# Two transformer blocks on one Trainium2 core: a quarter of the block sums by an adding DMA, transposes three steps later, rotations on VectorE

## The chip, the cores and the metric

The kernel runs on one core of one Trainium2 chip. The core has five engines that each work through their own instructions in order and wait for each other by semaphores: TensorE (PE: matmuls and transposes), VectorE (DVE), ScalarE (ACT), GpSimd (POOL) and SyncE (SP, which here only issues DMAs). The metric is the device time of one execution in microseconds; less is better.

## What is computed

256 tokens of width 1024 go through two blocks of two layers each, all in fp32. Each layer is a gated feed-forward net, a token mixer, and a second feed-forward net, so there are eight feed-forward nets; the first block normalises with layer_norm, the second with rms_norm. The part that the change touches most is the feed-forward net, and of the second block's mixer the rotary step on the attention's queries and keys:

```python
def swiglu(x, w13, w2):
    a, b = jnp.split(x @ w13, 2, axis=-1)
    return (jax.nn.silu(a) * b) @ w2

def partial_rotary(t, positions):
    half = ROPE_DIM // 2
    ...
    t1 = t[..., :half].astype(jnp.float32)
    t2 = t[..., half:ROPE_DIM].astype(jnp.float32)
    rot = jnp.concatenate([t1 * cos - t2 * sin, t2 * cos + t1 * sin], axis=-1).astype(t.dtype)
    return jnp.concatenate([rot, t[..., ROPE_DIM:]], axis=-1)

def first_block(x, ...):
    ...
    for l in range(DEPTH):
        x = layer_norm(ALPHA * x + 0.5 * swiglu(x, ffn1_w13[l], ffn1_w2[l]), ln_g[l, 0], ln_b[l, 0])
        m = mixer(x, w_in[l], ...)
        x = layer_norm(ALPHA * x + m, ln_g[l, 1], ln_b[l, 1])
        x = layer_norm(ALPHA * x + 0.5 * swiglu(x, ffn2_w13[l], ffn2_w2[l]), ln_g[l, 2], ln_b[l, 2])
    return x
```

## The kernel before

**Tiling.** The tokens are two streams, i = 0 and 1, of 128 tokens. A product with weights is made of three matmuls in fp32r: each weight tile w is split into a rounded part wh and a rest wl, each input into xh and xl, and wh·xh, wl·xh and wh·xl are added up in one PSUM bank (128 x 512 fp32). Weights come as units of 128 x 1024 (512 KB). For each unit, `fetch` (L225) has SP load it four units ahead, and `split` (L258) has ACT round it to wh (L270) and DVE subtract to get wl (L273), a few units ahead of PE.

**A feed-forward net** is 84 units. The first two groups of hidden columns are computed for each stream on its own (`group`, L316), the rest for both streams together (`joint`, L455), and three *pairs* of groups stand among them (`pair`, L487). A pair multiplies a 2 x 2 block matrix of inputs (two streams, two halves of the width) by a 2 x 2 block matrix of weights ("11", "12", "21", "22") by the Strassen-Winograd scheme: seven products instead of eight, in the order p1, p2, q5, p3, p6, p7, q4, of two units and 12 matmuls (L545) each. There are 24 pairs in the program, three in each of the eight nets. The weights of four products are sums of blocks:

- q5 = p1's block + "12", p6 = q5 + "22", p7 = "22" + "12", q4 = p6 + "21".

`sum` (L240) makes each of them with one DVE add of 128 x 1024 a unit (L246), in place, when the unit before has been split: 8 adds a pair, 192 in all. The raw blocks, wh and wl are slots of one ring of 24 tiles (`whp`).

Between the products stand rows of the second weight matrix (`on`, L478, its matmuls at L300 into the banks called big), after p1, q5, p6 and p7 as given by `GAPS`. There are four PSUM banks for groups and products (pool `grp`): p1, p2 and q5 take one each; p3 adds on in q5's bank, and p6, p7 and q4 in p1's. So `after` (L519) copies a result with ACT (L499) before its bank is used again, and adds p2's bank into the copy of p1 with DVE (L502).

**Order around the change.** `later(n, fn)` puts `fn` off by n ticks of a clock that counts the units; with it, the transposes of what a group (`hidden`, sg, L438 to L449) or a pair (`hidden` within `pair`, kp, L509) has made are placed TURNS = 4 ticks later. In the attention's `rot` (L1011), POOL computes the rotation in six operations (L1021 to L1026) on queries aq and keys ak, and the transposes come 5 ticks later. SP and POOL work in the order of the program; the instructions of PE, DVE and ACT are put in order by a scheduler.

Of the kernel before, what the change touches and what calls it, by code (L numbers as in the profile page):

```python
# [11 lines left out]
F32 = mybir.dt.float32  # L12
# [3 lines left out]
ALU = mybir.AluOpType  # L16
# [3 lines left out]
P = 128  # L20
# [16 lines left out]
RAMP = 3  # L37
STEP = 1
TAIL = 2
PAIR = 5  # L40
LAGS = dict(ffn=9, mixer1=6, mixer2=6)
STAGES = 4
# [11 lines left out]

OWN = 2

TURNS = 4
FFN = (("g", 8), ("s", 2, 0, 1, 2, 3), ("g", 9), ("s", 4, 16, 17, 4, 5), ("g", 10), ("s", 6, 6, 7, 18, 19),
       ("r", 8), ("r", 9), ("r", 20), ("r", 21))
LAST = (10, 11, 12, 13, 14, 15)  # L60
# [19 lines left out]
class Core:  # L80
# [5 lines left out]
    def __init__(self, ctx, tc, a, out, order):  # L86
        self.tc, self.nc, self.a, self.out = tc, tc.nc, a, out
        self.order = order
        p = lambda n, b, **k: ctx.enter_context(tc.tile_pool(name=n, bufs=b, **k))
        self.cp = p("cp", 1)  # L90
        self.stg = p("stg", STAGES)
        self.whp = p("whp", 2 * RING)
        self.sp = p("sp", SLOTS)
        self.vp = p("vp", 2)
        self.st = p("st", 12)
        self.big = p("big", 4, space=PSUM)
        self.grp = p("grp", 4, space=PSUM)


        self.phase, self.made = [], []  # L100
        at = 0
        for what, _ in order:
            mixer = ("mixer1", 56) if what == "b1" else ("mixer2", 36)
            for kind, made in (("ffn", _ffn_units()), (mixer[0], list(range(mixer[1]))), ("ffn", _ffn_units())):
                self.phase += [(kind, m) for m in range(len(made))]
                self.made += [m + at if isinstance(m, int) else (*m[:2], m[2] + at) for m in made]
                at += FFN_ROWS if kind == "ffn" else len(made)
        self.nunit = len(self.made)
        self.raw = {}
        self.next_dma = self.next_split = 0  # L110
        self.stages, self.units = {}, {}
        self.n = 0
        self.clock = 0
        self.queue = []
        self.pos = [0, 0]
        self.x = [None, None]
        self.sh = {}
# [88 lines left out]
    def lead(self):  # L206
# [3 lines left out]
        left = dict(ffn=len(_ffn_units()), mixer1=56, mixer2=36)[kind] - n  # L210
        if self.product(min(self.pos[0] + PAIR, self.nunit - 1)):
            return PAIR
        return LEAD + (MORE if n < FIRST else max(0, MORE - left // RAMP))
# [23 lines left out]
    def block(self, b, u, base):  # L237
        return self.a["ws"][base + 2 * BLOCKS.index(b) + u]

    def sum(self, p, u, base):  # L240


        raw = self.raw

        def add(t, other):
            self.nc.vector.tensor_add(t, t, other)  # L246
            raw[p, u, base] = t

        if p == "q5":
            add(raw.pop(("p1", u, base)), raw["12", u, base])  # L250
        elif p == "p6":
            add(raw.pop(("q5", u, base)), raw["p3", u, base])
        elif p == "p7":
            add(raw.pop(("p3", u, base)), raw.pop(("12", u, base)))
        elif p == "q4":
            add(raw.pop(("p6", u, base)), raw.pop(("p2", u, base)))

    def split(self, u):  # L258
        while self.next_split <= min(u, self.nunit - 1):
            v = self.next_split  # L260
            self.fetch(v)
            made = self.made[v]
            product = self.product(v)
            w = self.raw[made] if product else self.stages.pop(v)
            hi = self.whp.tile([P, 1024], F32R, tag="w", name=self.nm("wh"))
            lo = self.whp.tile([P, 1024], F32R, tag="w", name=self.nm("wl"))
            halves = [slice(0, 512), slice(512, 1024)]
            wide = v >= 8 and self.phase[v][0] == "ffn"
            for h, c in enumerate([slice(0, 1024)] if wide else halves):
                r = self.nc.scalar.activation(hi[:, c], w[:, c], AF.Copy)  # L270
                if v < 3:
                    self.pin(r)
                self.nc.vector.tensor_sub(lo[:, c], w[:, c], hi[:, c])  # L273
            self.units[v] = [hi[:, c] for c in halves], [lo[:, c] for c in halves]
            self.next_split += 1
            self.fetch(v + STAGES)
            if self.next_split < self.nunit and self.product(v + 1):
                self.sum(*self.made[v + 1])

# [51 lines left out]
    def rows(self, i, ks, xT, accs, first, last):  # L331
# [3 lines left out]
        for k in ks:  # L335
            wh, wl = self.units[self.pos[i]]
            xh, xl = xT(k)
            both = k <= last - TAIL
            cs = (0, 1) if both else (0,)
# [93 lines left out]
    def hidden(self, J, i, acc, g):  # L433
# [18 lines left out]

        self.later(TURNS, turn)

# [32 lines left out]
    def pair(self, J, g, ks):  # L487
# [20 lines left out]
        def hidden(i, t, sg):  # L508
# [7 lines left out]

            self.later(TURNS, turn)

# [446 lines left out]
    def mixer2(self, i, rs, l):  # L965
        nc = self.nc
# [44 lines left out]
        def rot(name, scale):  # L1011
            def f(acc):
                t = self.slot(name=name)
                nc.scalar.activation(t, acc, AF.Identity, scale=rs)
                r = t.rearrange("p (h d) -> p h d", h=8)[:, :, 0:16].rearrange("p h (two e) -> p h two e", two=2)
                t1, t2 = r[:, :, 0, :], r[:, :, 1, :]
                cs = self.con[:, C_COS + 8 * i:C_COS + 8 * i + 8].unsqueeze(1).to_broadcast([P, 8, 8])
                sn = self.con[:, C_SIN + 8 * i:C_SIN + 8 * i + 8].unsqueeze(1).to_broadcast([P, 8, 8])
                w = self.slot((P, 4, 8, 8), name="rw")
                g = nc.gpsimd  # L1020
                g.tensor_tensor(w[:, 0], t1, cs, op=ALU.mult)  # L1021
                g.tensor_tensor(w[:, 1], t2, sn, op=ALU.mult)
                g.tensor_tensor(w[:, 2], t2, cs, op=ALU.mult)
                g.tensor_tensor(w[:, 3], t1, sn, op=ALU.mult)
                g.tensor_tensor(t1, w[:, 0], w[:, 1], op=ALU.subtract)
                g.tensor_tensor(t2, w[:, 2], w[:, 3], op=ALU.add)  # L1026

                def turn():
                    tp = self.transposed(t)
                    o = self.slot(name=name + "T")  # L1030
                    nc.scalar.activation(o, tp, AF.Copy, scale=scale)
                    J[name, i] = o

                self.later(5, turn)
            return f

        def av(acc):
# [424 lines left out]
def _ffn_units():  # L1462


    out, n = list(range(4 * OWN)), 4 * OWN
    for what, _, *ks in FFN:
        if what == "s":
            base, gaps = n, GAPS[len(GAPS) - len(ks):]
            n += 8
            for p in PRODUCTS:  # L1470
                out += [(p, u, base) for u in range(2)]
                if p in gaps:
                    out.append(n)
                    n += 1
        else:
            m = 4 if what == "g" else 1
            out += range(n, n + m)
            n += m
    return out + list(range(n, n + len(LAST)))
# [120 lines left out]
```

## Time and profile before

| | us |
|---|---|
| median of three runs | 2153.34 (2152.36 to 2153.6) |
| profiled execution | 2151.26 |
| its span, first to last instruction | 2149.5 |
| mean granted TensorE clock | 0.996 |
| PE busy | 2103.2 |
| DVE busy | 1849.6 |
| ACT busy | 1329.9 |
| POOL busy | 248.3 |
| DMA | 394.52 MB, 52.8% of the 16 engines' span |

How to read it: the span is the time from the first instruction to the last; the profiled execution's own time is longer by what lies around that. An engine's idle time costs something only where another engine waits for its next result. The granted clock is the share of full speed (2.4 GHz) that TensorE was given; 0.50 is the lower level, 1.2 GHz. A wait in the list of waits is idle time of an engine just before an instruction, put down to the line whose result came last. Times in the rows are microseconds from the span's start, and a row of the timeline gives the start and the duration of an instruction, or of several of one kind together (x4), and in brackets the idle time before it.

### The profile page before, as it was taken

What the parts mean: (1) busy time and instruction counts of PE and PEld (TensorE: products, weight loads), DVE (VectorE), ACT (ScalarE), POOL (GpSimd) and SP (SyncE); (2) the same over time, 40 slices, a digit from 0 to 9 for tenths busy, and PEclk for the clock granted to TensorE, in tenths of its full rate; (3) what the DMA queues carried; (4) which work ended last, traced back from release to release, by engine and by line L of the source; (5) the groups of instructions that cost most, each with busy time, mean ns of one, the idle gap of its engine ahead of it and who ended that gap; (6) DMA issues with size and microseconds to landing.
All of it is one profiled execution on the core that took longest, in us unless ns stands there. A gap on an engine that the chain in (4) does not pass through costs nothing.

```text
span 2149.5 us, 27945 instructions
## 1 busy us (share of the span) xinstructions
PE 2103.2 (98%) x9904; PEld 1730.3 (80%) x9904; DVE 1849.6 (86%) x2532; ACT 1329.9 (62%) x2040; POOL 248.3 (12%) x269
## 2 busy tenths in 40 slices
PE   8999999999999999999999999999999999999998
PEld 7887878888888887888888788788778878788887
DVE  7997787998899878699989988679988998777995
ACT  6665754666466575466656666756566666666663
POOL 0000420000000033001100201510200110241000
PEclk9999999999999999999999999999999999999999
DMA  8556455465554744546556454525554546343552
GB/s 313 187 191 239 138 184 172 161 240 193 200 194 177 232 154 164 189 163 228 194 195 216 176 196 133 177 98 197 208 196 173 186 181 211 122 158 117 204 189 98
DMA packets 115292, 394.52 MB, mean 184 GB/s; under 512 B 12880, under 2 KB 15312, under 8 KB 115152
## 3 DMA queue, kind: packets, MB, share of 16 engines
q1 hardware_dynamic: 115152, 392.73, 52.8%
q8 instruction: 78, 1.28, 0.2%
q14 instruction: 62, 0.51, 0.1%
HBM read 391.63 MB, written 1.05 MB: 183 GB/s over the span
## 4 chain that ended last, share of the span: by engine, by line
PE 81%; DVE 5%; issue 2%; ACT 2%; POOL 1%; DVEq 0%; POOLq 0%; ACTq 0%
PE g L300 32%; PE big L300 24%; PE g L545 18%; PE g L284 3%; DVE wl L273 2%; PE big L1254 1%; PE big L1283 1%; POOL rw L1021 1%; DVE raw L246 0%; ACT wh L270 0%; ACT xh L308 0%; PE big L1167 0%; PE big L1201 0%; PE big L793 0%; PE big L1173 0%
## 5 line engine op out<-in xcount | busy, mean ns | idle before, releaser
L273 DVE TENSOR_TENSOR wl<-stg,wh 128x512 fp32r<-128x512 f32 (+1 forms) x712 | 666.3, 957 | 122.6 <-ACT wh L270 114.1
L270 ACT ACTIVATE wh<-stg 128x512 fp32r<-128x512 f32 (+1 forms) x712 | 565.0, 823 | 222.2 <-DMA stg<-in_ws_dram 82.1
L300 PE MATMUL g<-wh,xh 128*128 128x512 f32 x1184 | 480.2, 406 | 9.6 <-ACT wh L270 5.6
L270 ACT ACTIVATE wh<-raw 128x1024 fp32r<-128x1024 f32 x336 | 352.3, 1058 | 196.9 <-DVE raw L246 106.6
L300 PE MATMUL g<-wl,xh 128*128 128x512 f32 x1184 | 464.9, 393 | 0.0
L300 PE MATMUL g<-wh,xl 128*128 128x512 f32 x1184 | 462.6, 392 | 0.7 <-DVE xl L309 0.7
L273 DVE TENSOR_TENSOR wl<-raw,wh 128x1024 fp32r<-128x1024 f32 x336 | 415.6, 1251 | 28.4 <-ACT wh L270 26.2
L300 PEld LDWEIGHTS g<-wh,xh 128*128 128x128 f32 x1184 | 223.5, 189 | 56.7 <-ACT xh L308 5.7
L300 PEld LDWEIGHTS g<-wh,xl 128*128 128x128 f32 x1184 | 223.4, 189 | 49.7 <-DVE xl L309 1.5
L300 PEld LDWEIGHTS g<-wl,xh 128*128 128x128 f32 x1184 | 224.0, 189 | 42.3 <-DVE wl L273 0.8
L246 DVE TENSOR_TENSOR raw<-raw,raw 128x1024 f32<-128x1024 f32 x192 | 233.0, 1231 | 5.5 <-DMA raw<-in_ws_dram 5.0
L300 PE MATMUL big<-wh,hT 128*128 128x512 f32 x640 | 183.9, 391 | 0.0
L545 PE MATMUL g<-wh,Xh 128*128 128x512 f32 x384 | 151.0, 394 | 1.7 <-ACT kp L499 1.4
L545 PE MATMUL g<-wl,Xh 128*128 128x512 f32 x384 | 150.2, 391 | 0.0
L545 PE MATMUL g<-wh,Xl 128*128 128x512 f32 x384 | 149.1, 390 | 0.0
L300 PEld LDWEIGHTS big<-wh,hT 128*128 128x128 f32 x640 | 119.5, 188 | 24.6
L300 PE MATMUL big<-wh,hTh 128*128 128x512 f32 x384 | 123.9, 390 | 0.0
L300 PE MATMUL big<-wh,hTl 128*128 128x512 f32 x384 | 123.8, 390 | 0.0
L300 PE MATMUL big<-wl,hTh 128*128 128x512 f32 x384 | 123.5, 389 | 0.0
L545 PE MATMUL g<-wh,xh 128*128 128x512 f32 x288 | 115.4, 401 | 0.0
L408 POOL TENSOR_TENSOR m<-m,nhalf 128x1 f32<-128x1 f32 (+1 forms) x24 | 25.5, 1065 | 761.2 <-DVE m L407 761.2
L545 PE MATMUL g<-wl,xh 128*128 128x512 f32 x288 | 113.1, 393 | 0.0
(319 smaller groups left out, 3045.0 us busy)
## 6 DMA issues: line engine op xcount, KB each, us to landing
stg<-in_ws_dram SPq DMA_DIRECT2D x519, 512.0 KB, 4.3
raw<-in_ws_dram SPq DMA_DIRECT2D x192, 512.0 KB, 4.7
row<-in_norm_gain_dram SPq DMA_DIRECT2D x24, 256.0 KB, 6.1
row<-in_ln_g_dram SPq DMA_DIRECT2D x12, 256.0 KB, 4.8
row<-in_ln_b_dram SPq DMA_DIRECT2D x12, 256.0 KB, 6.4
xT<-in_xT_dram SPq DMA_DIRECT2D x4, 256.0 KB, 5.9
x<-in_x_dram SPq DMA_DIRECT2D x4, 256.0 KB, 8.5
out_dram<-x SPq DMA_DIRECT2D x4, 256.0 KB, 2.0
```

The costliest lines, as they stand in the source:

```text
L246: self.nc.vector.tensor_add(t, t, other)
L270: r = self.nc.scalar.activation(hi[:, c], w[:, c], AF.Copy)
L273: self.nc.vector.tensor_sub(lo[:, c], w[:, c], hi[:, c])
L284: self.nc.tensor.transpose(tp[:, hs(j)], src[:, hs(j)], self.ident)
L300: self.nc.tensor.matmul(accs[c], a, b[c], start=start and q == 0, stop=stop and q == 2)
L408: self.nc.gpsimd.tensor_tensor(out, out, self.nhalf[:, 0:n], op=ALU.pow)
L545: nc.tensor.matmul(bank[p], x[:, hs(k)], w[j], start=first[p] == p and k + q == 0, stop=k == 3 and q == 2, skip_group_check=True)
L1021: g.tensor_tensor(w[:, 0], t1, cs, op=ALU.mult)
L1254: nc.tensor.matmul(ps[:, hh * S + j * P:hh * S + j * P + P], J["aq", i][r, hs(head // 2)], J["ak", j][r, hs(head // 2)], start=True, stop= ...
L1283: nc.tensor.matmul(o[:, 64 * hh:64 * hh + 64], pT[:, hs(2 * hh + j)], J["av", j][:, head * 64:head * 64 + 64], start=j == 0, stop=j == 1)
```

## The change

1. `added` is new. For each unit of p7, twelve units ahead (EARLY), SP loads block "12" into a tile of its own in the ring, and a DMA on POOL's queue adds block "22" to it from DRAM. The DVE adds of p7 go. q5 and p6 now give the raw blocks "12" and "22" back to the ring, since p7 doesn't use them.
2. TURNS goes from 4 to 7, for sg and kp.
3. The six operations of `rot` go from POOL to DVE, and their transposes come 4 ticks later instead of 5.

```diff
+EARLY = 12
...
-TURNS = 4
+TURNS = 7
...
+    def added(self, v):
+        if self.product(v) and self.made[v][0] == "p7":
+            _, u, base = self.made[v]
+            t = self.raw[self.made[v]] = self.whp.tile([P, 1024], F32, tag="w", name=self.nm("sum"))
+            self.nc.sync.dma_start(t, self.block("12", u, base))
+            self.nc.gpsimd.dma_start(t, self.block("22", u, base), accum_op=ALU.add)
...
         if p == "q5":
-            add(raw.pop(("p1", u, base)), raw["12", u, base])
+            add(raw.pop(("p1", u, base)), raw.pop(("12", u, base)))
         elif p == "p6":
-            add(raw.pop(("q5", u, base)), raw["p3", u, base])
-        elif p == "p7":
-            add(raw.pop(("p3", u, base)), raw.pop(("12", u, base)))
+            add(raw.pop(("q5", u, base)), raw.pop(("p3", u, base)))
...
             self.fetch(v + STAGES)
+            while self.next_sum < min(v + EARLY, self.nunit):
+                self.added(self.next_sum)
+                self.next_sum += 1
             if self.next_split < self.nunit and self.product(v + 1):
                 self.sum(*self.made[v + 1])
...
-                g = nc.gpsimd
+                g = nc.vector
...
-                self.later(5, turn)
+                self.later(4, turn)
```

In the changed kernel the lines past `split` are 11 further down (L545 is L556, L502 is L513), those ahead of it 2 to 10.

What it does to the order is shown at three places. The first is PE in one pair of the first net (g_5407 and g_5413 hold the transposes of sg, L284 before and L295 after; the products are at L545, now L556; g_5429 is p1's bank before, g_5447 and g_5484 are p2's and q5's now). Before, the transposes stand ahead of p1:

```order
L300 MATMUL big_5165<-wh_5320,hT_5272 128x512
L300 MATMUL big_5166<-wh_5320,hT_5272 128x512
L284 MATMUL g_5407<-con,sg_5363 128x128 x2
L284 MATMUL g_5413<-con,sg_5366 128x128 x2
L545 MATMUL g_5429<-wh_5326,xh 128x512
L545 MATMUL g_5429<-wl_5327,xh 128x512
```

and with the change between p2 and q5:

```order
L556 MATMUL g_5447<-wl_5375,xh 128x512
L556 MATMUL g_5447<-wh_5374,xl 128x512
L295 MATMUL g_5467<-con,sg_5393 128x128 x2
L295 MATMUL g_5473<-con,sg_5396 128x128 x2
L311 MATMUL big_5092<-wh_5437,hT_5224 128x512
L311 MATMUL big_5093<-wh_5437,hT_5224 128x512
L311 MATMUL big_5092<-wl_5438,hT_5224 128x512
L556 MATMUL g_5484<-wh_5399,Xh_5227 128x512
```

The transposes moved past p1 and p2 and took three matmuls of a row with them; before, q5's first matmul followed p2's last.

The second is SP's queue in a pair, from the load of "21" to that of "22" (raw is a block, stg a row's unit, sum the tile of the sum). Before:

```order
L234 DMA raw_4083<-in_ws_dram 128x1024
L234 DMA raw_4089<-in_ws_dram 128x1024
L234 DMA raw_4130<-in_ws_dram 128x1024
L231 DMA stg_4136<-in_ws_dram 128x1024
L234 DMA raw_4154<-in_ws_dram 128x1024
L234 DMA raw_4179<-in_ws_dram 128x1024
```

With the change:

```order
L236 DMA raw_4099<-in_ws_dram 128x1024
L236 DMA raw_4105<-in_ws_dram 128x1024
L236 DMA raw_4137<-in_ws_dram 128x1024
L247 DMA sum_4139<-in_ws_dram 128x1024
L233 DMA stg_4146<-in_ws_dram 128x1024
L247 DMA sum_4148<-in_ws_dram 128x1024
L236 DMA raw_4176<-in_ws_dram 128x1024
L236 DMA raw_4201<-in_ws_dram 128x1024
```

The two loads of "12" for the sum stand ahead of the loads of "22" (the last two rows), one on each side of the row's unit.

The third is the rotation of one stream's queries, before on POOL (rw and aq are its tiles):

```order
L1007 MEMSET vx_12067 128x4x4
L1021 TENSOR_TENSOR rw_12141<-aq_12139,con 128x64
L1022 TENSOR_TENSOR rw_12141<-aq_12139,con 128x64
L1023 TENSOR_TENSOR rw_12141<-aq_12139,con 128x64
L1024 TENSOR_TENSOR rw_12141<-aq_12139,con 128x64
L1025 TENSOR_TENSOR aq_12139<-rw_12141 128x8x8
L1026 TENSOR_TENSOR aq_12139<-rw_12141 128x8x8
```

and now on DVE:

```order
L281 TENSOR_TENSOR wl_12180<-stg_12051,wh_12179 128x512 x2
L1032 TENSOR_TENSOR rw_12201<-aq_12199,con 128x64
L1033 TENSOR_TENSOR rw_12201<-aq_12199,con 128x64
L1034 TENSOR_TENSOR rw_12201<-aq_12199,con 128x64
L1035 TENSOR_TENSOR rw_12201<-aq_12199,con 128x64
L281 TENSOR_TENSOR wl_12213<-stg_12091,wh_12212 128x512
L1036 TENSOR_TENSOR aq_12199<-rw_12201 128x8x8
L1037 TENSOR_TENSOR aq_12199<-rw_12201 128x8x8
L281 TENSOR_TENSOR wl_12213<-stg_12091,wh_12212 128x512
```

They stand among the subtractions that make wl (L281) and share their queue.

## Rows read from the trace of the kernel before

**Rows 1.** The page, part 1: busy time of each engine.
```profile
PE 2103.2 (98%) x9904; PEld 1730.3 (80%) x9904; DVE 1849.6 (86%) x2532; ACT 1329.9 (62%) x2040; POOL 248.3 (12%) x269
```
**Rows 2.** List of waits, PE: line, releaser, us in total, times, longest.
```profile
PE g L284 <- POOL aq L1026: 6.6, 2, 3.3
...
PE g L284 <- DVE kp L509: 5.1, 3, 2.1
PE g L284 <- DVE sg L443: 4.6, 3, 1.9
...
PE g L284 <- DVE sg L440: 1.7, 2, 0.9
```
**Rows 3.** Timeline, PE: start us, us, engine, line, operation, tiles [idle before].
```profile
1206.12 0.63 PE L284 MATMUL g<-con,kp 128*128 128x128 f32 x4 [2.07 <-DVE kp L509]
```
**Rows 4.** Windows at half clock: us, busy of each engine, clock, DMA share, GB/s.
```profile
1348.65:1352.06 3.41, 2.72 (x8) 1.92 (x8) 0.00 (x0) 0.60 (x1) 2.31 (x8) 0.50 0.31 118
1570.52:1573.93 3.41, 3.41 (x10) 2.64 (x9) 2.65 (x5) 1.47 (x3) 0.00 (x0) 0.50 0.00 0
1870.89:1881.13 10.24, 8.62 (x21) 6.03 (x22) 3.39 (x6) 5.15 (x11) 4.96 (x13) 0.50 0.36 120
```
**Rows 5.** Windows in one pair, busy of PE, PEld, DVE, ACT, POOL.
```profile
434.00:446.00 12.00, 12.00 (x57) 9.75 (x56) 11.43 (x13) 8.43 (x10) 0.00 (x0) 1.00 0.95 375
...
454.00:474.00 20.00, 20.00 (x92) 16.54 (x91) 19.97 (x21) 14.83 (x20) 0.00 (x0) 1.00 0.24 82
```
**Rows 6.** Groups by line and form, DVE: busy us, mean ns | idle before.
```profile
L246 DVE TENSOR_TENSOR raw<-raw,raw 128x1024 f32<-128x1024 f32 x192 | 233.0, 1231 | 5.5 <-DMA raw<-in_ws_dram 5.0
...
L1286 DVE TENSOR_SCALAR at<-big,m 128x64 f32<-128x64 f32 x32 | 8.2, 279 | 6.5 <-PE big L1283 6.3
```
**Rows 7.** Timeline, SP's DMA queue: the row unit's load in that pair.
```profile
440.06 0.36 SPq L231 DMA_DIRECT2D stg<-in_ws_dram  x1
```
**Rows 8.** DMA issues of 430 to 446: count, KB each, median us to landing.
```profile
raw<-in_ws_dram SPq DMA_DIRECT2D x7, 512.0 KB, 7.8
```
**Rows 9.** Timeline, ACT: q5's copy and a rounding in that pair.
```profile
465.09 0.60 ACT L499 ACTIVATE kq<-g 128x512 f32<-128x512 f32 x1 [0.96 <-PE g L545]
466.97 1.06 ACT L270 ACTIVATE wh<-raw 128x1024 fp32r<-128x1024 f32 x1 [1.28 <-DVE raw L246]
```
**Rows 10.** Timeline, PE: the first matmul of p3 in that pair.
```profile
467.61 0.39 PE L545 MATMUL g<-wh,Xh 128*128 128x512 f32 x1
```
**Rows 11.** Timeline, PE, another pair: transposes of sg, then p2 to its end.
```profile
501.24 0.60 PE L284 MATMUL g<-con,sg 128*128 128x128 f32 x4
501.60 0.49 PE L545 MATMUL g<-wh,xh 128*128 128x512 f32 x1
501.92 0.39 PE L545 MATMUL g<-wl,xh 128*128 128x512 f32 x1
...
504.23 0.39 PE L545 MATMUL g<-wh,xl 128*128 128x512 f32 x1
```
**Rows 12.** Timeline, DVE, the same pair: the add that frees p2's bank.
```profile
504.80 0.68 DVE L502 TENSOR_TENSOR kp<-kp,g 128x512 f32<-128x512 f32 x1
```
**Rows 13.** Timeline, PE, a third pair: p2's last matmul.
```profile
1187.36 0.39 PE L545 MATMUL g<-wh,xl 128*128 128x512 f32 x1
```
**Rows 14.** Timeline, DVE, the third pair: the add that frees p2's bank.
```profile
1189.41 0.67 DVE L502 TENSOR_TENSOR kp<-kp,g 128x512 f32<-128x512 f32 x1
```
**Rows 15.** Timeline, POOL: the first two operations of a rotation.
```profile
1340.82 5.87 POOL L1021 TENSOR_TENSOR rw<-aq,con 128x64 f32<-128x64 f32 x1 [9.15 <-ACT aq L1014]
1346.66 0.31 POOL L1022 TENSOR_TENSOR rw<-aq,con 128x64 f32<-128x64 f32 x1
```
**Rows 16.** Timeline, DVE, at the end of that first operation.
```profile
1344.63 1.88 DVE L273 TENSOR_TENSOR wl<-stg,wh 128x512 fp32r<-128x512 f32 x3
1346.87 0.68 DVE L1116 TENSOR_TENSOR Gl<-gG,Gh 4x512 fp32r<-4x512 f32 x1 [0.36 <-ACT Gh L1115]
```
**Rows 17.** Timeline, POOL: a gating product in a net.
```profile
1011.83 8.13 POOL L568 TENSOR_TENSOR gr<-row,row 128x512 f32<-128x512 f32 x1 [83.89 <-PE big L300]
```

More of the change, by code (lines that the diff above doesn't have):

```diff
@@ L109, in __init__ @@
         self.raw = {}
-        self.next_dma = self.next_split = 0
+        self.next_dma = self.next_split = self.next_sum = 0
         self.stages, self.units = {}, {}
```

## Prediction

> **What bounds the kernel now.** Read the busy shares first: TensorE (PE) is busy 2103.2 us of a span of 2149.5, 98% [rows 1], so no change that leaves its matmuls alone can win more than its idle time and what it loses to a lower clock. The change removes no matmul and adds none. So the second view is PE's list of waits [rows 2]. Four of its lines come from transposes put into PE's order too soon after what they transpose: the rotated queries, made on GpSimd (POOL), 6.6 us in 2 waits; a pair's gated product kp 5.1 in 3; the same thing of an ordinary group, sg, 4.6 in 3 and 1.7 in 2. Together 6.6 + 5.1 + 4.6 + 1.7 = 18.0 us. One kp wait in the timeline shows their form: the transposes start at 1206.12 after 2.07 us of idling for VectorE (DVE) [rows 3], and every matmul behind them waits too, because PE takes its work in order. The third view is the granted clock in stretches: after the two waits for rotated queries and after the longest sg wait the clock is 0.50, the lower of the two levels, with 2.72, 3.41 and 8.62 us of PE work in it [rows 4]. That work would take half as long at full clock: 14.75 / 2 = 7.4 us. These stretches begin at such waits, so I count the clock's loss with them, though the third has other short idle times of its own that may keep it. The last thing to see is where DVE is full: 20 us in the middle of a pair have DVE busy 19.97 us, with the DMA engines at 0.24 [rows 5], while the 12 us before have DMA at 0.95.
>
> **Part 1, the sums by DMA.** Removed: 2 units x 24 pairs = 48 adds of 1231 ns on DVE [rows 6], 59.1 us. DVE doesn't release PE at those places, so this gives nothing of its own; it shortens the DVE queue that kp, sg and the bank add stand in, and I count it there. Added: 48 loads on SP and 48 adding DMAs on POOL's queue, 512 KB each, 50 MB in all. Their price on the DMA side is hidden if each sum is complete when ScalarE (ACT) rounds it to wh. Work it out in one pair. The second unit's sum load stands behind the stg load that SP issues at 440.06 [rows 7]; loads in this stretch land a median 7.8 us after their issue [rows 8], and two more stand in the queue, so the load lands at about 450. When must the sum be there? In the new order ACT rounds both units just ahead of the copy of q5's result, which stands at 465.09 and takes 0.60 us, and a rounding takes 1.06 [rows 9]; p3, which needs that copied bank, starts on PE at 467.61 [rows 10]. 467.61 - 0.60 - 1.06 = 466: the adding DMA may take 16 us from 450 before PE waits. No row shows an adding DMA. Bounds: nothing at the low end; at the high end the nearest transfer, 7.8 us, behind a POOL that is held. I take about 8 us, in a stretch with three quarters of the DMA time free [rows 5], so cost 0. If that cover fails, each microsecond beyond 16 costs 24, one for each pair. The raw blocks "12" and "22" are let go earlier and the sum holds a slot longer; PE and ACT want no slot sooner than 21 us (95 matmuls) after its release in the new order, so I cost the ring at 0.
>
> By the Trainium skill, "DMA: Bandwidth & Descriptors", section "Anatomy of one DMA — SWDGE (gpsimd) path", a GpSimd DMA takes 2.0 us plus its bytes over 436 GB/s, an estimate of 3.2 us for 512 KB; that is for plain copies, no run here shows one, and the sum would be the same.
>
> **Part 2, the transposes later.** TURNS 7 lets PE do more before it wants sg or kp. In the order there were 18 to 34 matmuls between a group's last matmul and its transposes, now 36 to 52; for kp 18 to 36, now 36. At 0.23 us a matmul (501.92 to 504.23 is ten of them [rows 11]) the cover grows from 4.1 us to 8.3. The longest wait of this kind was 2.1 us [rows 2], less than the 4.1 added, so I take kp, sg and sg to zero but for 10%: -11.4 + 1.1. Users of the transposed blocks still stand 42 or more matmuls behind. What is late next: the sg transposes now lie between p2 and q5 and hold two of four banks, so q5 must take p2's bank, which is free only when DVE has added p2's result. In 11 of 24 pairs only four transposes and three matmuls lie between; the other 13 have 4 to 12. Cover after p2's last matmul begins: 0.23 for itself, 0.36 for the transposes (501.24 to 501.60), 0.32 for the first matmul behind them (501.60 to 501.92), and two of 0.23: 1.37 us, or 0.98 past its end, since it lasts 0.39 [rows 11]. Need: the add ends at 504.80 + 0.68 where the matmul ended at 504.23 + 0.39, so 0.86 [rows 11, 12]; the worst pair ended at 1189.41 + 0.67 where the matmul ended at 1187.36 + 0.39, so 2.33 [rows 13, 14]. Bounds for the 11 pairs: 0, and 11 x (2.33 - 0.98) = 15 us. The typical pair is near 0.86 and a few near 1.2, and DVE has fewer adds: I take 11 x 0.12 = 1.3.
>
> **Part 3, the rotations.** Six operations for each of eight tiles, 48 in all, of 128x64; DVE does one of that size in 279 ns [rows 6], so at most 13.4 us on DVE, well under the 59.1 freed. On POOL the first took 5.87 us and the next 0.31 [rows 15]; it ended as DVE, which worked back to back, had its first idle time of 0.36 us, before 1346.87 [rows 16]. So POOL was held by DVE and not slow. This is the row on which the gain of 6.6 rests: on DVE the operation waits for at most one or two weight roundings. The Trainium skill, "SBUF — State Buffer", section "Who interferes with whom", says that a DVE instruction with two inputs in SBUF contends with a GpSimd one that reads SBUF, one blocking the other fully; the trace agrees, 5.87 against 0.31 us.
>
> The transposes come at the same time a step earlier (4 for 5): the order has 18 to 34 matmuls ahead of them where it had 24 to 42. At the four tightest, cover is 18 x 0.23 = 4.1 us against a chain of ACT copy 0.6 [rows 9], six operations 1.7 [rows 6], and one or two roundings between them, 3.5 to 5: 0 to 0.9 each, 0 to 3.6 in all; I take 1.5.
>
> **Sum**, against the profiled execution (2151.26 us, its span and what lies around it): -18.0 - 7.4 + 1.1 + 1.3 + 1.5 = -21.5, so 2129.8. The median of the runs stands 2.1 above that execution, so **2132**. With its own bounds: all waits gone and some of the small DVE waits too, 2123; clock not given back and the bank wait half of its bound, 2143.
>
> **Rivals.**
> 1. *q5's bank.* The add after p2 comes late in most pairs, as in [rows 13, 14], because a weight rounding of 1.2 us now stands ahead of it: 15 us in the 11 pairs and some 5 in the other 13, so 2132 - 1.3 + 20 = 2151. For it: DVE is full there [rows 5]. Against: the usual 0.86. Time 2143 to 2157, mostly no change.
> 2. *Slower: POOL held.* The adding DMA is issued by POOL, and if what it does there is held by gapless DVE work as the rotation was for 5.87 us [rows 15], or the gating product for 8.13 [rows 17], the sums are late. Decisive is 16 us behind the load. One held is 450 + 8.1 + 7.8 = 465.9, just nothing. Both held one after the other: 474, 8 us past 466 in each pair, x 24 = 192, so about 2324. For it: DVE busy 19.97 of 20. Against: the two holds are the longest of the trace, and DVE has fewer operations now. The Trainium skill, "SBUF — State Buffer", same section, gives this as a stall of GpSimd-issued DMAs under certain DVE operations, and infers that a two-input add or subtract is not among them; no run here shows either.
> 3. *More.* A freer DVE also takes the small waits of PE away: under 2123.
> 4. *The stalls move.* The waits are shared out again behind later transposes, and the clock falls elsewhere: within 4 us of 2153.
>
> **Numbers.** A measurement of this kernel tells about 0.2% (4.3 us) from no change. Forecast 0.60; rival 1 0.15 (faster 0.05, same 0.09, slower 0.01); rival 2 0.13; rival 3 0.07; rival 4 0.05. Faster 0.60 + 0.05 + 0.07 = 0.72; same 0.09 + 0.05 = 0.14; slower 0.13 + 0.01 = 0.14. The range leaves out rival 2 and rival 3, 0.20, and reaches from 2121 to the end of rival 1, 2156.
>
> **What would show it.** Right: no aq line in PE's waits; kp and sg under 2 us together; full clock in the places of [rows 4]; POOL with 48 operations fewer and DVE lower by some 46 us; sums landing over 5 us before ACT rounds them. Rival 1: PE waiting for DVE's add (L513) at q5. Rival 2: ACT waiting for the adding DMA ahead of its roundings, 24 times, and PE behind the q5 copy. The forecast is wrong if PE's total wait doesn't fall by more than 10 us.

## The result, and the profile after

The changed kernel takes 2187.59 us (median of four runs, 2183.98 to 2190.17) against 2152.85 for the kernel before: a ratio of 1.0162, 95% interval 1.0146 to 1.0178. It is 35 us slower; 2132 was forecast.

One correction to the section on the change: in its first pair of fences g_5429 is p2's bank, so the transposes stood ahead of p2, not of p1, and they moved past p2 alone; the three matmuls behind them belong to the row that stood after q5 before. The prediction's sums, which go by p2's end, use the right places.

The profiled execution's span grew from 2149.5 to 2188.4. The first lines of the page, to be held against [rows 1]:

```profile
span 2188.4 us, 28137 instructions
## 1 busy us (share of the span) xinstructions
PE 2118.5 (97%) x9904; PEld 1739.8 (79%) x9904; DVE 1799.7 (82%) x2532; ACT 1331.9 (61%) x2040; POOL 245.5 (11%) x269
```

PE has the same 9904 instructions. Its idle time, span less busy, went from 46.3 to 69.9 us (+23.6), and its busy time from 2103.2 to 2118.5 (+15.3) at a mean granted clock of 0.989 instead of 0.996. The two make up the 38.9 us. DVE is 50 us less busy, as the change meant, and the kernel is slower.

The list of waits on PE (line, releaser, us in total, times, longest), which answers to [rows 2]:

```profile
PE g L556 <- DVE kp L513: 37.7, 13, 6.7
...
PE g L295 <- DVE sg L454: 3.6, 3, 1.3
...
PE g L295 <- DVE sg L451: 2.1, 1, 2.1
...
PE g L295 <- DVE aq L1037: 0.7, 2, 0.4
```

The 18.0 us of [rows 2] shrank to 6.4, and kp's transposes wait for nothing. In their place stands a wait at q5 (L556) for DVE's add of p2's bank (L513), 37.7 us. Where does the add's delay come from? DVE's own list of waits, one row:

```profile
DVE raw L256 <- DMA raw<-in_ws_dram: 67.4, 40, 4.0
```

Before, the same line (L246) waited 5.0 us for loads [rows 6]. Of the 67.4 us, 38.8 in 17 of the 24 pairs are waits for the second load of block "22", 22.8 for the first. The chain can be followed in one pair whose p2 ends at 977.28. First SP's queue and POOL's (start, duration, queue, line, operation):

```profile
955.88 0.33 SPq L247 DMA_DIRECT2D sum<-in_ws_dram  x1
956.31 0.37 SPq L233 DMA_DIRECT2D stg<-in_ws_dram  x1
957.47 0.33 SPq L247 DMA_DIRECT2D sum<-in_ws_dram  x1
960.46 3.32 SPq L236 DMA_DIRECT2D raw<-in_ws_dram  x2
```

```profile
961.23 0.95 POOL L248 DMA_DIRECT2D sum<-in_ws_dram  x1 [19.51 <-ACT hT L459]
964.91 0.86 POOL L248 DMA_DIRECT2D sum<-in_ws_dram  x1 [2.73 <-DMA sum<-in_ws_dram]
```

The raw x2 at 960.46 are the two loads of block 22; the first adding DMA starts beside them. The DMA issues of that stretch (count, KB each, median us to landing), after the change:

```profile
raw<-in_ws_dram SPq DMA_DIRECT2D x2, 512.0 KB, 6.9
sum<-in_ws_dram POOLq DMA_DIRECT2D x1, 512.0 KB, 8.2
```

and the same two loads in the kernel before (946.6 to 950.0 of its time):

```profile
raw<-in_ws_dram SPq DMA_DIRECT2D x2, 512.0 KB, 3.9
```

Over all 24 pairs the second load of 22 takes a median 8.0 us from issue to landing where it took 3.4, and lands 5.9 us before p2's end where it landed 11.1. DVE's timeline in this pair shows what that does:

```profile
971.41 1.23 DVE L256 TENSOR_TENSOR raw<-raw,raw 128x1024 f32<-128x1024 f32 x1 [1.91 <-DMA raw<-in_ws_dram]
972.56 1.22 DVE L281 TENSOR_TENSOR wl<-stg,wh 128x1024 fp32r<-128x1024 f32 x1
973.69 0.42 DVE L451 SCALAR_TENSOR_TENSOR sg<-g,sg 128x256 f32<-128x256 f32 x1
974.03 4.81 DVE L281 TENSOR_TENSOR wl<-raw,wh 128x1024 fp32r<-128x1024 f32 x4
978.76 1.22 DVE L256 TENSOR_TENSOR raw<-raw,raw 128x1024 f32<-128x1024 f32 x1
979.89 0.68 DVE L513 TENSOR_TENSOR kp<-kp,g 128x512 f32<-128x512 f32 x1
```

The row at 971.41 is p6's second sum; it waits for that load. From there DVE works without a gap, one sum, one sg, five wl and a sum of q4, until the bank add begins at 979.89. So in this pair each microsecond by which the load is late is one by which the add is late. Over all pairs the add ends a median 3.3 us behind p2's end, where it was 0.9. And PE, in the same pair:

```profile
977.12 0.60 PE L295 MATMUL g<-con,sg 128*128 128x128 f32 x4
977.47 0.71 PE L311 MATMUL big<-wh,hT 128*128 128x512 f32 x2
978.02 0.40 PE L311 MATMUL big<-wl,hT 128*128 128x512 f32 x1
980.63 0.79 PE L556 MATMUL g<-wh,Xh 128*128 128x512 f32 x1 [2.21 <-DVE kp L513]
```

Four transposes, three matmuls, then 2.21 us of idling, and then the lower clock (window from 981.2 to 983.9; its granted clock is the 0.50):

```profile
981.20:983.90 2.70, 2.70 (x8) 2.10 (x7) 2.70 (x4) 1.93 (x3) 0.00 (x0) 0.50 0.20 33
```

### The profile page after: what moved, and what is told of

Its sections match the earlier page's. It is cut to its first block, busy times and chain, and to the rows that moved or that the text cites. A ratio compares the mean times of both kernels' runs of the same rounds, so it can differ in the third digit from the quotient of the medians.

```text
span 2188.4 us, 28137 instructions
## 1 busy us (share of the span) xinstructions
PE 2118.5 (97%) x9904; PEld 1739.8 (79%) x9904; DVE 1799.7 (82%) x2532; ACT 1331.9 (61%) x2040; POOL 245.5 (11%) x269
## 3 DMA queue, kind: packets, MB, share of 16 engines
q0 software_dynamic: 6912, 25.17, 6.3%
## 4 chain that ended last, share of the span: by engine, by line
PE 57%; DVE 5%; issue 2%; DMA 2%; ACT 2%; POOL 0%; DVEq 0%; POOLq 0%; ACTq 0%
PE g L311 22%; PE big L311 17%; PE g L556 13%; DVE wl L281 3%; PE g L295 2%; DMA raw<-in_ws_dram 2%; PE big L1265 1%; PE big L1294 1%; DVE raw L256 0%; PE big L1212 0%; PE big L1178 0%; PE big L1184 0%; ACT xh L319 0%; ACT wh L278 0%; DVE qk L1144 0%
## 5 line engine op out<-in xcount | busy, mean ns | idle before, releaser
L281 DVE TENSOR_TENSOR wl<-stg,wh 128x512 fp32r<-128x512 f32 (+1 forms) x712 | 658.5, 948 | 135.8 <-ACT wh L278 127.7
L311 PE MATMUL g<-wl,xh 128*128 128x512 f32 x1184 | 463.2, 391 | 0.0
L278 ACT ACTIVATE wh<-raw 128x1024 fp32r<-128x1024 f32 x288 | 300.2, 1057 | 177.1 <-PE g L311 70.3
L281 DVE TENSOR_TENSOR wl<-raw,wh 128x1024 fp32r<-128x1024 f32 x288 | 353.7, 1246 | 29.8 <-ACT wh L278 16.9
L256 DVE TENSOR_TENSOR raw<-raw,raw 128x1024 f32<-128x1024 f32 x144 | 180.1, 1252 | 67.6 <-DMA raw<-in_ws_dram 67.4
L556 PE MATMUL g<-wh,Xh 128*128 128x512 f32 x384 | 159.1, 416 | 40.1 <-DVE kp L513 37.7
L556 PE MATMUL g<-wl,Xh 128*128 128x512 f32 x384 | 156.7, 408 | 0.0
L556 PE MATMUL g<-wh,Xl 128*128 128x512 f32 x384 | 156.2, 407 | 0.0
L311 PEld LDWEIGHTS big<-wh,hT 128*128 128x128 f32 x640 | 118.5, 188 | 23.6
L556 PEld LDWEIGHTS g<-wh,Xh 128*128 128x128 f32 x384 | 76.3, 199 | 64.9 <-DVE kp L513 43.6
L248 POOL DMA_DIRECT2D sum<-in_ws_dram x48 | 42.0, 874 | 695.4 <-DVE wl L281 260.0
L556 PE MATMUL g<-wh,xh 128*128 128x512 f32 x288 | 114.8, 398 | 0.0
```

The source lines that it names most:

```text
L248: self.nc.gpsimd.dma_start(t, self.block("22", u, base), accum_op=ALU.add)
L311: self.nc.tensor.matmul(accs[c], a, b[c], start=start and q == 0, stop=stop and q == 2)
L556: nc.tensor.matmul(bank[p], x[:, hs(k)], w[j], start=first[p] == p and k + q == 0, stop=k == 3 and q == 2, skip_group_check=True)
```

## The experiments

The theory drawn from these rows, called joint in the expectations: q5 takes p2's bank, and DVE frees it late because it stood waiting for block 22, which the adding DMAs delay. Twelve kernels were run, on four chips; times are medians of runs, ratios against the kernel before on the same chip with 95% intervals.

**The parts alone.** TURNS alone:

```diff
-TURNS = 4
+TURNS = 7
```

> The kernel before with TURNS 7 and nothing else: sums on VectorE, rotations on GpSimd. Joint theory (q5 has to take p2's bank, and the add that frees it is late because it stands behind p6's second sum, which waits for a load of block 22 that the adding DMAs delay): the bank is p2's here too, but the load of 22 lands about 11 us before p2's end as before, so the wait for the add stays under 12 us in all, and the kp and sg waits (11.4 us) go: 2138 to 2153. Rival A (the later transposes alone cost the time): over 25 us of waiting for the add, 2175 or more.

2152.49 us, 0.9995 (0.9986 to 1.0004). The bank add was waited for 2.7 us in 3 places, so the detour to p2's bank costs little by itself, and rival A falls. But there was also no gain: kp's waits went, and sg's at L443 grew from 4.6 to 7.2 us:

```profile
PE g L284 <- DVE sg L443: 7.2, 3, 2.6
PE g L284 <- POOL aq L1026: 6.6, 2, 3.3
...
PE g L545 <- DVE kp L502: 2.7, 3, 0.9
```

The three waits for the bank stand in the pairs in which kp was waited for before. The three for sg (L443) stay where they were, although the order has 49 PE instructions between the group's last matmul and these transposes where it had 34. DVE's timeline at one of the three places shows why, first before, then with TURNS 7:

```profile
1569.66 0.42 DVE L443 TENSOR_TENSOR sg<-g,sg 128x256 f32<-128x256 f32 x1
```

```profile
1570.38 0.42 DVE L443 TENSOR_TENSOR sg<-g,sg 128x256 f32<-128x256 f32 x1
```

The group's last matmul ends at 1560.72 and 1557.33, so the product that is waited for is done 9.4 us behind it before and 13.5 with TURNS 7. The scheduler, which orders DVE as well, has put nine operations of DVE instead of six between the group's two sg products. So the cover grew, and the product moved back with it.

The rotations alone:

```diff
-                g = nc.gpsimd
+                g = nc.vector
...
-                self.later(5, turn)
+                self.later(4, turn)
```

> The kernel before with the rotations on VectorE and their transposes at 4, nothing else. By the prediction's part 3 the two waits of 6.6 us go and with them most of the half-clock stretches after them (2 to 5 us): 2139 to 2147. Rival G (without the freed 59 us of VectorE the rotation is as late there): 2150 to 2156.

2142.67 us, 0.9953 (0.9938 to 0.9968): the 10 us that were expected, and rival G falls. PE's list has 0.7 us left for aq, PE's busy time is 2100.2 (3.0 less, the lower clock's share) and its idle time 39.9 (6.4 less). The kp and sg waits stand as they were (5.2 and 4.6).

Rotations and TURNS 7 together, the change with the sums left on DVE:

> Rotations on VectorE and TURNS 7, sums on VectorE as before. If the parts add up, TURNS 7 gives nothing and the rotations some 10 us: 2139 to 2149; the distance from here to the kernel without adding DMAs (2131.7) is what taking 48 adds from VectorE is worth. Rival G: 2150 or more.

2140.87 us, 0.9943 (0.9928 to 0.9958). TURNS 7 adds 2 us to the gain, within the intervals of both. The waits for sg and the bank remain: 6.6 us for sg (L443) in 3 places, 2.6 for the add in 3.

Rotations and the later transposes for kp alone:

```diff
-            self.later(TURNS, turn)
+            self.later(7, turn)
```

> Rotations on VectorE, and TURNS 7 for a pair's kp alone (sg stays at 4, so q5 doesn't take p2's bank); sums on VectorE as before. The kp waits (5.2 us in the kernel with the rotations alone) go, the sg waits (4.6) stay: 2134 to 2141. Rival (the later transposes only move the wait to the next product of VectorE): 2141 to 2146.

2141.19 us, 0.9955 (0.9941 to 0.9970), the lower edge of the rival, and no gain over the rotations alone (0.9953): kp's waits went, 5.0 us for hT (L449) at the products came, and sg's (L443) grew from 4.6 to 6.2. While DVE is as full as before, the waits taken from one of its products came back at others.

**The adding DMAs.** TURNS back at 4 in the changed kernel:

```diff
-TURNS = 7
+TURNS = 4
```

> The changed kernel with TURNS back at 4: sums by adding DMA, rotations on VectorE. Joint theory: the load of 22 still lands 5 us later than before and VectorE still waits for it, but q5 doesn't take p2's bank, so nobody waits for the add: the rotation waits (6.6 us) and their clock loss go, kp and sg waits stay or grow some us as VectorE is late: 2140 to 2158. Rival B (the adding DMAs alone cost the time, whatever the bank): 2175 or more.

2169.64 us, 1.0072 (1.0048 to 1.0096): between both theories, and a miss for the joint one. q5 doesn't take p2's bank here, and the loss is still 27 us over the rotations alone. The load of 22 takes 8.0 us as in the changed kernel, DVE waits 51.1 us for loads, and PE waits for what DVE owes it next:

```profile
PE g L556 <- DVE hT L460: 18.3, 12, 2.5
PE g L295 <- DVE sg L454: 7.1, 4, 3.1
PE g L295 <- DVE kp L520: 6.8, 5, 2.1
```

So the bank isn't the cause but the dearest place to be late at. Between TURNS 7 and 4 lie 18 us with the adding DMAs (2187.6 and 2169.6) and -2 with the sums on DVE (2140.9 and 2142.7).

The changed kernel without the adding DMAs:

```diff
-            self.nc.gpsimd.dma_start(t, self.block("22", u, base), accum_op=ALU.add)
```

> The changed kernel without the 48 adding DMAs; their 48 loads of block 12 stay, so the sum lacks block 22. Joint theory: the load of 22 lands 9 to 11 us before p2's end instead of 5.9, VectorE doesn't wait for it, PE's wait for the add falls from 37.7 to under 12 us: 2133 to 2153. Rival C (the longer transfer list, the ring or VectorE's new order delay the add, not the adding DMA): waits stay above 25 us, 2172 or more.

2131.74 us, 0.9892 (0.9875 to 0.9908), 56 us below the changed kernel, and 0.3 from the forecast. The second load of 22 takes 4.5 us and DVE never waits for it; it waits 20.1 us for other loads, and PE's waits for sg and the bank add are small:

```profile
PE g L555 <- DVE kp L512: 2.7, 5, 0.8
...
PE g L294 <- DVE sg L453: 0.5, 1, 0.5
```

The order of PE, DVE and ACT is the same in both traces, operation by operation, and TURNS, the ring and the 48 added loads are all still there, so rival C falls. DVE's own work isn't slower beside the adding DMAs either: busy 1799.7 us with them, 1799.8 without. Against the kernel with rotations and TURNS 7 it is 9 us better (11 by the ratios, as the two ran on different chips), and PE's waits for sg are what goes: that is what 48 adds fewer on DVE are worth.

The adding DMAs as plain ones, with the same bytes on the same queue:

```diff
-            self.nc.gpsimd.dma_start(t, self.block("22", u, base), accum_op=ALU.add)
+            self.nc.gpsimd.dma_start(t, self.block("22", u, base))
```

> The changed kernel with the 48 adding DMAs turned into plain ones: the same bytes, queue and places, block 22 overwrites block 12 in the sum's tile, so the sum is left out. Theory D (an adding transfer costs more than its bytes: it delays the loads beside it because it adds): block 22's second load lands 8 to 11 us before p2's end, and the time is 2130 to 2150. Rival E (the 25 MB more on GpSimd's queue are enough): the load lands later than 7 us before p2's end and the time is 2170 or more.

2139.85 us, 0.9946 (0.9928 to 0.9964), again with the same order on PE, DVE and ACT. So of the 56 us the bytes and the queue cost about 8, and the adding about 48 (12 and 47 by the ratios, as the kernels ran on different chips). DVE waits 29.2 us for loads, 1.7 of it for the second load of 22, and PE 7.2 for the bank add. The DMA queues of the two runs say the same (packets, MB, share of 16 engines' span); first with adding:

```profile
q0 software_dynamic: 6912, 25.17, 6.3%
```

and plain:

```profile
q0 software_dynamic: 6912, 25.17, 3.2%
```

The same number of packets and bytes kept the DMA engines busy twice as long: 6.3% of 2188.4 us over 48 is 2.9 us of all 16 engines each, 3.2% of 2133.8 is 1.4. Landing takes a median 9.2 us against 7.3. The load of 22 beside them took 6.0 us and landed 8.1 before p2's end, between the 5.9 with adding and the 9.4 without. Why an added byte takes twice as long isn't shown by any run.

One unit of each p7 by adding DMA, the other on DVE:

```diff
-        if self.product(v) and self.made[v][0] == "p7":
+        if self.product(v) and self.made[v][0] == "p7" and self.made[v][1] == 0:
...
+        elif p == "p7" and u == 1:
+            add(raw.pop(("p3", u, base)), raw.pop(("12", u, base)))
```

> The changed kernel with the adding DMA for p7's first unit only; its second unit is summed on VectorE as before: 24 adding DMAs instead of 48. Theory D (the price is the time by which an adding DMA holds up the load of 22 beside it): half the adding transfers, and the load of 22 that matters lands 7.5 to 9.5 us before p2's end instead of 5.9, so most of the loss goes: 2132 to 2150. Rival H (any adding DMA in a pair costs the same, say by the wait of the queue): 2165 or more.

2145.89 us, 0.9978 (0.9965 to 0.9991): most of the loss goes, as theory D has it, but 24 adding DMAs still cost more than the 24 adds that they save (2140.9 without any).

**Other places for the adding DMAs.** With another EARLY the scheduler also gives PE, DVE and ACT another order (at EARLY 8, 276 of DVE's 2532 places hold another operation, at 18, 640, at 24, 508), so the next three runs don't change the place alone. EARLY 8, behind the loads of 22:

```diff
-EARLY = 12
+EARLY = 8
```

> The changed kernel with EARLY 8: SP issues the sums' loads behind both loads of 22, so the adding DMAs can't delay these. Joint theory: the load of 22 lands 9 to 11 us before p2's end, PE's wait for the add falls under 12 us; the sums land some 5 us later than with 12 and may be late by 0 to 2 us in some pairs: 2135 to 2165. Rival C (VectorE's order alone): as the changed kernel, 2175 or more.

2176.28 us, 1.0105 (1.0089 to 1.0121): the time is a miss, above the theory's range and inside rival C's. The delay of the load went all the same, which speaks against rival C's cause: the load of 22 takes 3.4 us again and PE no longer waits for the bank add. But the sums land just as ACT has stood waiting for them, one in the pair at 977 by 2.73 us, with the copy of q5 behind:

```profile
975.67 1.06 ACT L278 ACTIVATE wh<-sum 128x1024 fp32r<-128x1024 f32 x1 [0.39 <-DMA sum<-in_ws_dram]
979.46 1.06 ACT L278 ACTIVATE wh<-sum 128x1024 fp32r<-128x1024 f32 x1 [2.73 <-DMA sum<-in_ws_dram]
980.42 0.58 ACT L510 ACTIVATE kq<-g 128x512 f32<-128x512 f32 x1
```

PE waits for that copy:

```profile
PE g L556 <- ACT kq L510: 28.5, 21, 3.0
```

EARLY 18, ahead of the loads of 12 and 22:

```diff
-EARLY = 12
+EARLY = 18
```

> The changed kernel with EARLY 18: both sums' loads stand ahead of the loads of 12 and 22, and the adding DMAs run beside p1's, p2's and the first loads of 12. Theory D: block 22 lands 8 to 10 us before p2's end, but what is delayed is now q5's sum or an ordinary unit; 2138 to 2165, PE's wait for the bank add under 20 us. Rival (the place doesn't matter, each adding DMA costs its 1 us of PE): 2180 or more.

2182.86 us, 1.0138 (1.0110 to 1.0166): a miss, above the theory's range and inside that of the rival, by which the place doesn't matter. The second load of 22 takes 3.8 us, so it isn't held up, but blocks issued before it are: the first load of 12 takes a median 9.1 us where it took 4.4 in the changed kernel, and 34.1 of the 36.8 us that DVE waits for loads in its sums are waits for it. PE's waits are spread over the bank add (16.4), sg (9.7) and hT (4.3). EARLY 24, among the ordinary units:

```diff
-EARLY = 12
+EARLY = 24
```

> The changed kernel with EARLY 24: the adding DMAs run among the sparse loads of ordinary units, before a pair's eight block loads. Theory D with the joint theory: block 22 lands 9 to 11 us before p2's end, the sums are done over 15 us ahead, PE's wait for VectorE's bank add is under 10 us: 2128 to 2150. Rival F (adding DMAs delay whatever loads run beside them, here the ordinary units that ScalarE then waits for): 2160 or more.

2154.22 us, 1.0004 (0.9995 to 1.0014): between the theories and 29 us below EARLY 18, so the place, or the order that comes with it, does matter. DVE waits only 6.3 us for block loads, but ACT waits for the units that are loaded beside the adding DMAs, 141.7 us where it was 77.7 without adding DMAs:

```profile
ACT wh L278 <- DMA stg<-in_ws_dram: 141.7, 121, 4.9
```

Rival F is right in kind: what runs beside is delayed, here 33 us cheaper than at EARLY 12. Last, block 22 added from its copy in SBUF:

```diff
-            self.nc.gpsimd.dma_start(t, self.block("22", u, base), accum_op=ALU.add)
+            self.pending.append((t, u, base))
...
+            while self.pending and ("p3", *self.pending[0][1:]) in self.raw:
+                t, u, base = self.pending.pop(0)
+                self.nc.gpsimd.dma_start(t, self.raw["p3", u, base], accum_op=ALU.add)
```

> The changed kernel with the adding DMA's source changed: not block 22 in DRAM but the copy of it that SP has loaded for p3, so that an adding DMA can't begin before that load has landed and can't delay it. Theory D: block 22 lands 9 to 10 us before p2's end as without adding DMAs, VectorE's wait for it is about 20 us in all, PE's wait for the bank add is under 10 us; the sums land from 2 us before to 3 us after p2's end, just about when ScalarE rounds them: 2130 to 2152. Rival F (the adding DMA's cost doesn't depend on what it overtakes): 2160 or more.

2261.07 us, 1.0514 (1.0487 to 1.0541), a plain miss of the expected time and inside rival F's range. The load of 22 isn't delayed any more (DVE waits 20.3 us for loads, as without adding DMAs), but the adding DMAs take 10.0 us, begin later, and DVE waits for their end:

```profile
DVE wl L282 <- DMA sum<-raw: 82.1, 17, 6.7
...
PE g L560 <- DVE kp L517: 72.4, 17, 6.4
```

The sums aren't what is waited for: they land a median 5.2 us ahead of ACT's rounding, and the operation that waits makes a wl from a raw block. Counted through the ring of 24 tiles in the order in which the kernel takes them, the wl of q4's second unit gets the tile of the second block "22", which the adding DMA now reads to its end. That this reuse is the wait is a reading of the kernel and of the row; no run tests it. So the run can't decide between theory D and rival F.

The run shows one thing more: with nothing read from DRAM an adding DMA of 512 KB takes no less, 10.0 against 9.2 us.

## Why the prediction was wrong

**Right: what bounds the kernel, and part 3.** PE's waits and the lower clock behind them account for the time in every run compared here. For the rotations the sum has 6.6 us of waits, half of 2.72 + 8.62 for the clock and 1.5 given back, -10.8; the rotations alone gave 2142.67 against 2153.0, -10.3. The split is less exact than the sum: in the profiled executions PE's idle time fell by 6.4 us, where the sum has 5.1, and its busy time by 3.0, where it has 5.7 for the clock. DVE's queue didn't hold the rotations up: PE waits 0.7 us for them, and the first of the six operations takes 0.21 us there.

**Wrong, and it decided: part 1, "so cost 0".** The prediction asked one thing of the adding DMAs, whether each sum would be complete when ACT rounds it. It was: an adding DMA took 9.2 us, near the 8 assumed, and the second sum of a pair landed a median 6.7 us ahead of ACT's rounding. It didn't ask which loads share the DMA engines with them. The "three quarters of the DMA time free" are those of 454 to 474 [rows 5]; by its own numbers the adding DMAs began at about 450, and the window of the kernel before that begins there, which [rows 5] leave out, has the DMA engines full (their share is the 1.02):

```profile
450.00:454.00 4.00, 4.00 (x20) 3.29 (x19) 3.96 (x5) 1.96 (x3) 0.00 (x0) 1.00 1.02 414
```

SP's order in the section on the change shows the two loads of 22 right behind the sums' loads. The price of the adding DMAs was 56 us (2187.6 less 2131.7), about 48 of it for adding rather than copying.

**Wrong in size: part 1's relief and part 2's gain.** The text gave the 59.1 us taken from DVE nothing of their own and TURNS 7 the whole of the kp and sg waits, -11.4 + 1.1, by setting 4.1 us more of cover against a longest wait of 2.1. Measured, TURNS 7 alone gives nothing (0.9995) and beside the rotations 2 us, within the intervals: the waits for kp come back at the bank add, and those for sg stay because DVE makes sg later too. The 48 adds fewer give 9 us. Together that is 11 us, and the sum has 10.7 for these places (11.4 - 1.1 - 1.3, and half of 3.41 for the clock). So the split was wrong and the total right, which is luck, and the kernel without adding DMAs comes out at 2131.7 where 2132 was forecast.

**Rival 1 had the place, and not the price.** PE does wait for the add L513 at q5. The bound of 20 us came from adds that end 0.86 to 2.33 us behind p2's end [rows 11 to 14]; in the pair above it ends 979.89 + 0.68 - 977.28 = 3.3 behind, which is also the median of the 24 pairs, and the waits sum to 37.7 us, with 15.3 us more of busy time at the lower clock over the whole program that the bound left out. It assumed a DVE as punctual as before, but p6's second sum, eight operations ahead of the add, now waited for a load.

**Rival 2's reason was wrong.** POOL wasn't held by a busy DVE: an adding DMA's issue takes 0.86 us, a median 0.56 after its load has landed. Its second half, ACT waiting for a sum with q5's copy behind it, is what EARLY 8 shows. The Trainium skill, "SBUF — State Buffer", section "Who interferes with whom", infers that a two-input operation on DVE leaves the descriptors of a GpSimd DMA alone; these issues agree with it. The same skill's "DMA: Bandwidth & Descriptors", section "Anatomy of one DMA — SWDGE (gpsimd) path", gives an estimate of 3.2 us for a copy of this size. The plain ones on that queue took 7.3 us beside other loads, so the measurement decides.

The best versions are those that leave the sums on DVE: rotations on DVE, with TURNS 7 at 2140.9 us or without at 2142.7, 0.6% and 0.5% faster than the kernel before and about 2% faster than the changed one.

## What to carry to other kernels

A DMA put off the critical path is paid for by the loads beside it: before counting it as hidden, list what is in flight in its stretch, and what waits in order behind each of those landings. An engine that works in order passes on the lateness of one input to everything behind it, so look for the next product that the bounding engine needs from it, and expect that wait, not the one removed. Where a scheduler orders the engines, placing a user later can place its input later too: read the input's place in the new order before counting the cover. Moving work from an engine that is full in a stretch can pay though that engine releases nothing there by name: here 48 adds were worth 9 us.

## What the runs showed of the hardware

- An adding DMA of 512 KB kept the DMA engines busy twice as long as a plain one of the same packets (6.3% and 3.2% of the span for 25.17 MB) and landed in a median 9.2 us, the plain one in 7.3; with its source in SBUF instead of DRAM it landed in 10.0, though in another place.
- The ordinary load beside it (the second of block 22, median of 24) took 8.0 us, 6.0 beside a plain DMA on the same queue and 4.5 without either.
- Beside the adding DMAs DVE's operations took as long as without them: 1799.7 and 1799.8 us in all.
- A POOL operation of 128x64 took 5.87 us beside a DVE that worked without a gap and 0.31 when it began in a gap [rows 15, 16]; on DVE the first took a median 0.21.
